# A batched matrix product on one core: the order of the first two loads, and stores joined into three transfers

## The chip, the cores and the metric

The kernel runs on one core of a Trainium2 chip. The metric is the device time of one execution in microseconds (us); the times below are medians of several runs. One execution is also recorded by the hardware profiler; its views are what the text quotes.

## The reference

Thirty-two independent matrix products in float32:

```python
batch, dim_i, dim_j, dim_k = 32, 256, 512, 384
x: (batch, dim_i, dim_j)   y: (batch, dim_j, dim_k)
return np.einsum('bij,bjk->bik', x, y).astype(np.float32)
```

x has 16.8 MB, y 25.2 MB and the result 12.6 MB.

## The kernel before

**Groups.** The 32 products are done in N = 8 groups of Q = 4. Each group uses all 128 partitions: 32 partitions (`PQ`) for each of its four products. One load brings x of a group (2 MB, 16 KB to a partition), one load brings y (3 MB, 24 KB to a partition). Both have two buffers (`x_sb`, `y_sb`). All results of all groups have room of their own in `o_sb`, so that a store never stands in the way of a later group; a group's results are 12 KB to a partition.

**Steps of one group.** GpSimd (POOL in the profile) rounds x and y to 16 bits: x in two halves (`x_r`, line 124), y in two or four pieces (`y_r`, line 132). VectorE (DVE) transposes the rounded x in blocks of 32 (`xt_sb`, line 146). TensorE (PE) multiplies in tiles of 32 rows (line 207), four products side by side, into eight banks of PSUM (`o_ps`): NE = 2 halves of the rows, four banks each. ScalarE (ACT) and VectorE copy the banks into `o_sb` (line 155).

**The order.** All transfers are issued by SyncE (SP) on one queue, in the order of its program. Loads of x(0), y(0), x(1) and y(1) are issued at the start (line 74). For each later group n, SP waits until POOL has rounded both halves of x of group n - 2 and then issues x(n); it waits for the first half of x of group n - 1, which POOL does right after y of group n - 2, and then issues y(n) (lines 97 to 101). Only when all loads are issued does SP come to the stores (lines 102 to 108). The store of a group waits for a mark that PE sets in the second half of the next group, as by then the copies of the group are over; the last store waits for the copies themselves. The last line of SP waits for all the stores.

**POOL's order** is x then y in every group (lines 119 to 133). Before it overwrites a half of `x_r` it waits for `s_free`, with which VectorE says that it has transposed it; before a piece of `y_r`, for PE's marks in the group before. `s_cast` counts the rounded halves of x, `s_yr` the rounded pieces of y.

The functions that the change touches, and what calls them:

Of the kernel before, what the change touches and what calls it, by code (L numbers as in the profile page):

```python
# [11 lines left out]
Q = 4  # L12
NE = 2
STEP = 4
STRAIGHT = 2


@with_exitstack
def kernel(
# [11 lines left out]
    PQ = P // Q  # L31
# [4 lines left out]
    N = B // Q  # L36
    NC = T // STEP

    def sbuf(name, shape, dtype):
        return nc.alloc_sbuf_tensor(name, shape, dtype).ap()  # L40
# [3 lines left out]
    o_sb = sbuf("o_sb", [P, N, NE, H, K], F32)  # L44
# [12 lines left out]
    s_act = nc.alloc_semaphore("s_act")  # L57
    s_dve = nc.alloc_semaphore("s_dve")
    s_pe = nc.alloc_semaphore("s_pe")
    s_sp = nc.alloc_semaphore("s_sp")  # L60
    s_out = nc.alloc_semaphore("s_out")
# [4 lines left out]
    def load_x(n):  # L66
        src = x[n * Q : (n + 1) * Q].rearrange("g (p r) j -> (g p) r j", r=R)
        return nc.sync.dma_start(out=x_sb[n % 2], in_=src).then_inc(s_x[n], 16)

    def load_y(n):  # L70
        src = y[n * Q : (n + 1) * Q].rearrange("g (q t) k -> (g q) t k", t=T)
        return nc.sync.dma_start(out=y_sb[n % 2], in_=src).then_inc(s_y[n], 16)

    for ins in (load_x(0), load_y(0), load_x(1), load_y(1)):
        tc.no_tile_sem_insts.add(ins.ins.name)
    tc.close()
    tc.compile()  # L77
# [9 lines left out]
    def chunk_done(n, e, a):  # L87
        return (n * NE + e) * MARKS + (a + 1 if a < NC - 1 else MARKS)

    sp = nc.sync  # L90

    def store(n):
        dst = out[n * Q : (n + 1) * Q].rearrange("g (s f) k -> (g s) f k", s=PQ)
        src = o_sb[:, n].rearrange("p e h k -> p (e h) k")
        sp.dma_start(out=dst, in_=src).then_inc(s_out, 16)

    for n in range(2, N):
        sp.wait_ge(s_cast, NE * (n - 1))
        load_x(n)
        sp.wait_ge(s_cast, NE * (n - 1) + 1)  # L100
        load_y(n)
    for n in range(N):
        if n < N - 1:
            sp.wait_ge(s_pe, chunk_done(n + 1, NE - 1, 0))
        else:
            sp.wait_ge(s_act, NE)
            sp.wait_ge(s_dve, NE)
        store(n)
    sp.sem_inc(s_sp, 1)
    sp.wait_op(s_out, 16 * N, "sem-ge").then_inc(s_out, -16 * N)  # L110

    def pieces(n):
        w = 1 if n in (0, N - 2, N - 1) else 2
        return [(a, a + w) for a in range(0, NC, w)]

    po = nc.gpsimd
    for n in range(N):
        po.wait_ge(s_x[n], 16)  # L120
        for e in range(NE):
            if n:
                po.wait_ge(s_free, max(2 * n - 2 + e, 1))
            po.tensor_copy(  # L124
                x_r[:, e], x_sb[n % 2][:, e * H : (e + 1) * H]
            ).then_inc(s_cast, 1)
        po.wait_ge(s_y[n], 16)
        for a, b in pieces(n):
            if n:
                po.wait_ge(s_pe, chunk_done(n - 1, NE - 1, b - 1))  # L130
            s = slice(a * STEP, b * STEP)
            ins = po.tensor_copy(y_r[:, s], y_sb[n % 2][:, s])  # L132
            ins.then_inc(s_yr, b - a if b < NC else b - a + NC)
    po.wait_ge(s_sp, 1)
    po.sem_clear(range(nums[0], nums[-1] + 1))

# [48 lines left out]
    def scalar_half(n, e):  # L185
        for g in range(Q - 1):
            a_.wait_ge(s_pe, bank_done(n, e, g))
            blocks = [b for b in BLOCKS[:-OWN] if b[0] == g]
            collect(a_.copy, n, e, blocks, None, s_act if g == Q - 2 else None)
# [3 lines left out]
    a_.sem_inc(s_act, NE)  # L193
    with a_.Fori(0, N - STRAIGHT) as n:
        with a_.Fori(0, NE) as e:
            scalar_half(n, e)
    for n in range(N - STRAIGHT, N):
        for e in range(NE):
# [7 lines left out]
    def product(ps, w, m, start, stop, g):  # L206
        return te.add_instruction(  # L207
            mybir.InstMatmult(
                name=nc.get_next_instruction_name(),
                start_tensor_calc=start,  # L210
                stop_tensor_calc=stop,
                tile_size=(PQ, P),
                tile_position=(PQ * g, 0),
                engine=mybir.EngineType.PE,
                ins=[te.lower_ap(m), te.lower_ap(w)],
                outs=[te.lower_ap(ps)],
            )
        )

    xt = xt_sb.bitcast(MM_DT).rearrange("p t (m c) -> p t m c", c=2)  # L220
    with te.Fori(0, N):
        with te.Fori(0, NE) as e:
            take(s_act)
            take(s_dve)
            for t in range(T):
# [3 lines left out]
                for g in range(Q):  # L229
                    s = slice(g * PQ, (g + 1) * PQ)  # L230
                    ins = product(
                        o_ps[:, e * Q + g, :K],
                        xt[s, t // 2, :, t % 2],
                        y_r[s, t],
                        t == 0,
                        t == T - 1,
                        g,
                    )
# [32 lines left out]
```

## Time and profile before

| | |
|---|---|
| median of three runs | 132.26 us (132.15 to 132.43) |
| the profiled execution | 132.16 us, its span 130.8 us |
| granted clock of TensorE, mean | 0.798 |
| bytes read and written in HBM | 41.94 MB and 12.58 MB |
| transfers issued | 8 of x, 8 of y, 8 of the result |

The span runs from the first to the last instruction; the execution's own time has some more around it. In the profile a row of the timeline has the start, the time from the first to the last of the instructions that it takes together, the engine, the line, the operation, the tile written and the tile read, their number, and in brackets the idle time of the engine before it and what ended that. "SPq" rows are transfers being issued. In a table of stretches the columns are the busy times of PE, PEld (weight load), DVE, ACT and POOL with their numbers of instructions, the granted clock, the mean share in which the 16 DMA engines had a packet, and the rate. A packet is counted where it starts.

### The profile page before, as it was taken

The page shows a single profiled execution, that of the slowest core. Times are in us where ns is not written, and L with a number is a line of the kernel's source. Part 1 is how long each engine was busy: PE and PEld are TensorE (multiplying, and loading weights), DVE is VectorE, ACT ScalarE, POOL GpSimd, SP SyncE. Part 2 cuts the span into 40 slices and gives each one's busy share as a digit, 9 for nine tenths or more (in the row PEclk, how much of TensorE's full clock was granted, in tenths as well). Part 3 has the DMA queues.
Part 4 walks back from the last instruction along what each step waited for, and adds up shares of the span by engine and source line. Part 5 has one row for each costly group of instructions (what it writes and reads, how often), then busy time and mean ns, then how long its engine had stood idle before and what let it go on. Part 6 is the DMA issues. An engine that isn't in the chain of part 4 may idle for free. (4 is left out here: it accounts for less than half of the span.)

```text
span 130.8 us, 3204 instructions
## 1 busy us (share of the span) xinstructions
PE 65.0 (50%) x1024; PEld 53.7 (41%) x1024; DVE 82.7 (63%) x144; ACT 84.3 (64%) x178; POOL 74.2 (57%) x42
## 2 busy tenths in 40 slices
PE   0000069903991698099529915980985499100000
PEld 0000057702990575089329505970963387000000
DVE  0006005897379989966998997589989957920000
ACT  0400000899359989993999899489999967995000
POOL 0047195499919955992899469758964970000000
PEclk9999999996589779756986995599599558965555
DMA  5999999999999999999999999999999999999996
GB/s 105 421 461 406 426 433 466 406 423 436 458 393 431 433 466 398 421 438 458 396 456 413 458 391 453 413 431 421 458 413 405 427 427 428 432 425 428 436 425 263
DMA packets 3459, 54.55 MB, mean 417 GB/s; under 512 B 384, under 2 KB 384, under 8 KB 384
## 3 DMA queue, kind: packets, MB, share of 16 engines
q1 hardware_dynamic: 3456, 54.53, 98.2%
q14 instruction: 3, 0.02, 0.0%
HBM read 41.94 MB, written 12.58 MB: 417 GB/s over the span
## 5 line engine op out<-in xcount | busy, mean ns | idle before, releaser
L155 ACT COPY o_sb<-o_ps (+1 forms) x176 | 82.8, 470 | 31.7 <-PE o_ps L207 29.5
L207 PE MATMUL o_ps<-y_r,xt_sb 32*128 32x384 f16 x1024 | 65.0, 406 | 46.7 <-PEq L204 46.5
L207 PEld LDWEIGHTS o_ps<-y_r,xt_sb 32*128 32x128 f16 x1024 | 53.7, 112 | 57.7 <-issue 52.2
L146 DVE STREAM_TRANSPOSE xt_sb<-x_r 128x256 f32<-128x256 f32 x64 | 38.2, 625 | 31.0 <-PE o_ps L207 20.3
L132 POOL CAST y_r<-y_sb 128x1536 f16<-128x1536 f32 (+1 forms) x22 | 44.3, 2049 | 8.0 <-DMA y_sb<-in_y_dram 7.8
L155 DVE COPY o_sb<-o_ps 32x384 f32 (+1 forms) x80 | 44.5, 557 | 1.6
L124 POOL CAST x_r<-x_sb 128x2048 f16<-128x2048 f32 x16 | 30.2, 1893 | 24.6 <-PE o_ps L207 8.3
L192 ACT ACT_TABLE_LOAD x1 | 1.3, 1283 | 3.5 <-PEq L77 3.5
L255 POOL MEMSET const-float32-0.0<- 128x1 f32 x1 | 0.1, 98 | 0.2 <-issue 0.2
L192 ACT COPY spare<-const-float32-0.0 1x1 f32<-1x1 f32 x1 | 0.2, 190 | 0.0
L255 POOL MEMSET const-bfloat16-1.0<- 128x1 bf16 x1 | 0.1, 101 | 0.0
L255 POOL MEMSET const-uint8-127<- 128x1 uint8 x1 | 0.1, 101 | 0.0
L255 POOL MEMSET const-float32-1.0<- 128x1 f32 x1 | 0.1, 98 | 0.0
## 6 DMA issues: line engine op xcount, KB each, us to landing
y_sb<-in_y_dram SPq DMA_DIRECT2D x8, 3072.0 KB, 16.9
x_sb<-in_x_dram SPq DMA_DIRECT2D x8, 2048.0 KB, 17.4
out_dram<-o_sb SPq DMA_DIRECT2D x8, 1536.0 KB, 24.6
```

Source lines behind the costliest of these rows:

```text
L124: po.tensor_copy(x_r[:, e], x_sb[n % 2][:, e * H : (e + 1) * H]).then_inc(s_cast, 1)
L132: ins = po.tensor_copy(y_r[:, s], y_sb[n % 2][:, s])
L146: v.transpose(xt_w[:, w], words[:, e, w]).then_inc(s_xt, 1)
L155: ins = copy(o_sb[g * PQ : (g + 1) * PQ, n, e, h], o_ps[h * PQ : (h + 1) * PQ, e * Q + g, :K],)
L192: a_.copy(spare, nc.const_aps.tensor(0.0, [1, 1], F32))
L207: return te.add_instruction(mybir.InstMatmult(name=nc.get_next_instruction_name(), start_tensor_calc=start, stop_tensor_calc=stop, tile_si ...
L255: nc = _bacc.Bacc("TRN2", target_bir_lowering=False, num_devices=1)
```

## The change

The first two loads change places: y of group 0 is issued ahead of x of group 0, and POOL rounds y of group 0 ahead of x of group 0. All other groups keep their order. On the side of the stores, the results of groups 0 to 4 go out in one transfer, those of groups 5 and 6 in a second, those of group 7 in a third. The first waits for the mark for which the store of group 4 waited, the second for that of group 6, the third for what the store of group 7 waited for.

```diff
+JOINED = 5
...
-    for ins in (load_x(0), load_y(0), load_x(1), load_y(1)):
+    for ins in (load_y(0), load_x(0), load_x(1), load_y(1)):
...
-    def store(n):
-        dst = out[n * Q : (n + 1) * Q].rearrange("g (s f) k -> (g s) f k", s=PQ)
-        src = o_sb[:, n].rearrange("p e h k -> p (e h) k")
-        sp.dma_start(out=dst, in_=src).then_inc(s_out, 16)
+    def store(first, last):
+        groups = out[first * Q : last * Q].rearrange("(n g) (s f) k -> (g s) n f k", g=Q, s=PQ)
+        src = o_sb[:, first:last].rearrange("p n e h k -> p n (e h) k")
+        sp.dma_start(out=groups, in_=src).then_inc(s_out, 16)
...
-    for n in range(N):
-        if n < N - 1:
-            sp.wait_ge(s_pe, chunk_done(n + 1, NE - 1, 0))
-        else:
-            sp.wait_ge(s_act, NE)
-            sp.wait_ge(s_dve, NE)
-        store(n)
+    sp.wait_ge(s_pe, chunk_done(JOINED, NE - 1, 0))
+    store(0, JOINED)
+    sp.wait_ge(s_pe, chunk_done(N - 1, NE - 1, 0))
+    store(JOINED, N - 1)
+    sp.wait_ge(s_act, NE)
+    sp.wait_ge(s_dve, NE)
+    store(N - 1, N)
     sp.sem_inc(s_sp, 1)
-    sp.wait_op(s_out, 16 * N, "sem-ge").then_inc(s_out, -16 * N)
+    sp.wait_op(s_out, 16 * 3, "sem-ge").then_inc(s_out, -16 * 3)
...
-    for n in range(N):
+
+    def round_x(n):
...
+    def round_y(n):
...
+    round_y(0)
+    round_x(0)
+    for n in range(1, N):
+        round_x(n)
+        round_y(n)
```

## The prediction

> **What bounds the kernel now.** I read the page first, its slices and its queue part.
>
> ```profile
> span 130.8 us, 3204 instructions
> PE 65.0 (50%) x1024; PEld 53.7 (41%) x1024; DVE 82.7 (63%) x144; ACT 84.3 (64%) x178; POOL 74.2 (57%) x42
> ...
> DMA  5999999999999999999999999999999999999996
> ...
> q1 hardware_dynamic: 3456, 54.53, 98.2%
> ...
> y_sb<-in_y_dram SPq DMA_DIRECT2D x8, 3072.0 KB, 16.9
> x_sb<-in_x_dram SPq DMA_DIRECT2D x8, 2048.0 KB, 17.4
> out_dram<-o_sb SPq DMA_DIRECT2D x8, 1536.0 KB, 24.6
> ```
>
> No computing engine is busy for more than two thirds of the span. The row of the DMA engines has a 9 in every slice but the first and the last, and the packets of the one queue fill 98.2% of sixteen engines' span. So the transfers are the bound, and what is left to ask is whether anything in between makes them wait. The chain of waits says the same in a roundabout way: it ends with ACT.
>
> ```profile
> by line: ACT o_sb L155 7.9%; PE o_ps L207 4.2%; issue 0.3%
> 45 pieces in order of time: start us, us, what
> ...
> 118.95 0.47 ACT o_sb L155
> ```
>
> The last piece of computing is over at 118.95 + 0.47 = 119.42 us, 11.4 us before the end of the span, and the chain explains only some 12% of it. The last 11.4 us are transfers that stand in line, the last store behind the earlier ones. A table of stretches shows how well the line is fed (columns: stretch and its length, busy time of the engines, granted clock, DMA share, GB/s).
>
> ```profile
> 0.00:1.70 1.70, 0.00 (x0) 0.00 (x0) 0.00 (x0) 0.00 (x0) 0.20 (x4) 1.00 0.00 0
> 1.70:5.00 3.30, 0.00 (x0) 0.00 (x0) 0.00 (x0) 1.47 (x2) 0.00 (x0) 1.00 1.02 318
> 5.00:28.00 23.00, 8.53 (x128) 6.87 (x128) 8.60 (x15) 4.50 (x10) 12.66 (x8) 1.00 1.00 432
> 28.00:98.00 70.00, 46.09 (x730) 39.26 (x734) 59.24 (x104) 59.47 (x127) 54.24 (x27) 0.78 1.01 431
> 98.00:102.00 4.00, 1.93 (x46) 1.18 (x37) 3.92 (x8) 3.88 (x10) 2.08 (x2) 0.99 0.94 400
> 102.00:118.00 16.00, 8.49 (x128) 6.40 (x128) 10.92 (x19) 13.54 (x30) 5.05 (x4) 0.71 1.01 427
> 118.00:126.00 8.00, 0.00 (x0) 0.00 (x0) 0.00 (x0) 1.40 (x3) 0.00 (x0) 0.50 1.01 430
> 126.00:129.50 3.50, 0.00 (x0) 0.00 (x0) 0.00 (x0) 0.00 (x0) 0.00 (x0) 0.50 1.00 428
> 129.50:130.80 1.30, 0.00 (x0) 0.00 (x0) 0.00 (x0) 0.00 (x0) 0.00 (x0) 0.50 0.05 19
> ```
>
> From 5 to 129.5 us the engines have a share of about 1.0 and carry 427 to 432 GB/s, except for four microseconds at 400 where the loads end and the stores begin. The span is then: 54.53 MB at 431 GB/s, 126.5 us; 1.70 us before the first packet; in 1.70 to 5 us 3.30 x (431 - 318) / 431 = 0.87 us lost to a slow start; by the same sum 0.29 us lost in 98 to 102 and 0.15 us in 102 to 118; and 1.30 x (431 - 19) / 431 = 1.24 us at the end. That makes 130.75 us beside a span of 130.8. The same execution took 132.16 us, 1.36 us more than its span; the median of the runs is 132.26 us, 0.1 above it, so I add or take off what the sum gives at 132.26. The three runs lie 0.28 us apart, about 0.2%: less than 0.26 us can hardly be told from no change here.
>
> **Part one: y of group 0 first.** No byte is added or removed; the first 5 MB come in another order. What could cost time is that work behind them comes later and with it the issues of later loads, since SP sends each only when POOL has rounded what held the buffer. The timeline of before, its rows of SP, POOL, DVE and PE:
>
> ```profile
> 0.74 0.38 SPq L68 DMA_DIRECT2D x_sb<-in_x_dram  x1
> ...
> 8.46 3.72 POOL L124 CAST x_r<-x_sb 128x2048 f16<-128x2048 f32 x2 [8.01 <-DMA x_sb<-in_x_dram]
> ...
> 12.21 0.33 SPq L68 DMA_DIRECT2D x_sb<-in_x_dram  x1
> ...
> 15.74 5.70 POOL L132 CAST y_r<-y_sb 128x1536 f16<-128x1536 f32 x4 [3.56 <-DMA y_sb<-in_y_dram]
> ...
> 17.66 8.53 PE L207 MATMUL o_ps<-y_r,xt_sb 32*128 32x384 f16 x128 [17.66 <-PEq L204]
> 19.66 0.64 DVE L146 STREAM_TRANSPOSE xt_sb<-x_r 128x256 f32<-128x256 f32 x1 [7.07 <-PE o_ps L207]
> ...
> 24.77 3.73 POOL L124 CAST x_r<-x_sb 128x2048 f16<-128x2048 f32 x2 [3.33 <-DVE o_sb L155]
> 26.69 0.33 SPq L72 DMA_DIRECT2D y_sb<-in_y_dram  x1
> ...
> 28.44 5.44 POOL L132 CAST y_r<-y_sb 128x3072 f16<-128x3072 f32 x2
> 28.53 0.33 SPq L68 DMA_DIRECT2D x_sb<-in_x_dram  x1
> ...
> 31.64 8.22 PE L207 MATMUL o_ps<-y_r,xt_sb 32*128 32x384 f16 x128 [5.46 <-PEq L204]
> ...
> 38.61 1.89 POOL L124 CAST x_r<-x_sb 128x2048 f16<-128x2048 f32 x1 [2.89 <-PE o_ps L207]
> ```
>
> In before, x of group 0 is in POOL's hands at 8.46 and y at 15.74. The two together are over at 15.74 whichever is first, since they share one line; y alone takes 15.74 - 8.46 = 7.28 us of it. After: y lands at about 8.46 + (7.28 - 4.9) = 10.9 (4.9 us is the x load, 2.10 MB at 431 GB/s), is rounded in 5.70 us until 16.6, and only then POOL takes x, which landed about 15.7: the halves are done at 18.4 and 20.3. DVE needs 0.64 us for the first transpose, so PE starts near 19.1 instead of 17.66. With all of y rounded it needn't wait for pieces any more; group 1 in before is such a group, and from PE's start to the POOL rounding that waits for its first half it took 38.61 - 31.64 = 6.97 us. So POOL takes x of group 1 at about 26.1 instead of 24.77, 1.3 us later.
>
> Each issue that hangs on this: x of group 2 goes out after both halves of x(0), at 20.3 instead of 12.21 (8.1 us later); y of group 2 after the first half of x(1), at 28.0 instead of 26.69; x of group 3 at 29.9 instead of 28.53; the later ones by at most as much. Do the engines run dry? The four loads sent at the start are 10.49 MB, so they end at about 1.70 + 0.87 + 10.49 / 0.431 = 26.9 us; x(2) at 20.3 is in line 6.6 us before that, and the first load needed 1.70 - 0.74, about 1.0 us, from issue to first packet. x(2) keeps the engines until 26.9 + 4.9 = 31.8; y(2) at 28.0 is 3.8 us early, 2.8 with that 1.0 us. It is hidden, and a slip of 2.8 us beyond the 1.3 would uncover it. Later loads have more cover: y(2) ends at 31.8 + 7.3 = 39.1, and x(3) is sent at 29.9. The compute of later groups waits for its loads (POOL rounds y of group 7 at 101.35 with "DMA y_sb" as the releaser, a row quoted below), so the 1.3 us are taken up on the way.
>
> What no row shows is a start with the bigger packets: 0.87 us are lost in 1.70 to 5 us with x's rows of 16 KB (2048 KB over 128 partitions), and y's rows have 24 KB. If the loss goes with the size, it grows to 1.30 (+0.44); if it goes with the number of packets, each carrying half as much again, it shrinks to 0.58 (-0.29). I take 0, because from 5 us on the rate is 432 with whatever packets are then under way: it looks like a spell of time. Both ends stay for the range.
>
> **Part two: three store transfers instead of eight.** The bytes are the same. SP's waits and issues near the stores, and the work that they wait for:
>
> ```profile
> 84.10 0.33 SPq L72 DMA_DIRECT2D y_sb<-in_y_dram  x1
> 84.47 2.33 SPq L95 DMA_DIRECT2D out_dram<-o_sb  x5
> ...
> 98.01 0.33 SPq L95 DMA_DIRECT2D out_dram<-o_sb  x1
> 109.84 0.33 SPq L95 DMA_DIRECT2D out_dram<-o_sb  x1
> 119.44 0.33 SPq L95 DMA_DIRECT2D out_dram<-o_sb  x1
> 101.35 5.70 POOL L132 CAST y_r<-y_sb 128x1536 f16<-128x1536 f32 x4 [1.92 <-DMA y_sb<-in_y_dram]
> ```
>
> The first five stores go out from 84.47 to 86.80, right behind the last load, and the one transfer of groups 0 to 4 waits for the mark of the fifth, which went out about 86.4: some 2 us later than the first store now. At that time the line holds the rest of y(6), x(7) and y(7), and the loads, 41.94 MB, end at 1.70 + 0.87 + 41.94 / 0.431 = 99.9 us. Cover: 13 us. The second transfer waits for the mark of store 6, at 109.84; groups 0 to 4, 7.86 MB at 428 GB/s, hold the engines from 99.9 until about 118.5, so it is 8.6 us early. Its group 5, which went out at 98.01, gains nothing from that and loses nothing. The third goes at 119.44 as now; groups 5 and 6 hold the line until 118.5 + 7.3 = 125.8, 6.4 us. Nothing else is queued on SP behind these waits, as all loads are sent. The last wait, for the three transfers' completion, ends with the last byte as before.
>
> What can change on the line itself are five boundaries between transfers fewer. No row times one, but stretches bound them: a store of 1.57 MB takes 3.66 us at 430 GB/s, and the stretches with only stores run at 427 to 430 where loads, with fewer boundaries, run at 431 to 432. If all the difference were the boundary, it costs (432 - 430) / 432 x 3.66 = 0.017 us at the least difference and 0.042 us at the largest. Five of them: 0.08 to 0.21 us; nothing, if the difference has another cause. I take 0.08, from the stretch of 118 to 126, where no computing engine disturbs.
>
> The joined transfer has another order of rows. A partition holds 12,288 bytes of each group next to one another, and in memory these lie one group (1.57 MB) apart; the store of one group instead fills memory with neighbouring rows. The Trainium skill's page "DMA: Bandwidth & Descriptors", section "Latency and other measured facts", has rates for copies whose partitions' rows lie at large powers of two: 207 GB/s at 512 KiB and 164 at 2 MiB. No trace here has such an access; an estimate by that page: at 164 GB/s the seven groups' 11.0 MB would take 67 us instead of 25.7. [...]
>
> **Sum.** 130.8 + 0 (start) - 0.08 (boundaries) + 0 (waits, all covered) = 130.7 of span; 132.26 - 0.08 = 132.2 us.
>
> **The rivals.** *Both unknowns help:* -0.29 at the start and -0.21 for the boundaries, 131.76 us. For it speaks that the 0.87 us are lost while few packets are on their way; against it, that the rate of store stretches dips for other reasons (427 while engines compute, 430 when they don't). Chance 0.24, with the milder mixtures past 0.26 us.
>
> *The slow start grows with the packet:* +0.44 - 0.08, 132.62 us, slower than before. It decides as soon as the loss at the start passes 0.87 + 0.34 = 1.21 us. For it: a first packet that creeps has half as many bytes again to creep with. Against it: the rate after 5 us shows nothing of packet size. Chance 0.12.
>
> *The hops between groups slow the stores:* if the two joined transfers, 11.01 MB, go at the 400 GB/s that is the lowest rate of a full line in the table (98 to 102 us), they take 27.5 us instead of 25.7 at 428: +1.8, 134.0 us. It passes 0.26 + 0.08 us at a rate under 423. Chance 0.05; by the skill's rule it would be far more.
>
> *The line runs dry before y(2):* needs the 2.8 us of slip worked out above, and costs what is slipped beyond it; 1 us gives 133.2. Nothing in the rows of PE or POOL is that uneven. Chance 0.03.
>
> *The change does nothing:* the joined transfers cut into the same packets, boundaries for free, 132.26 us; it is inside the forecast.
>
> **How the numbers follow.** Forecast within 0.26 us of before: 0.56, around 132.2 (its own range is 132.0 to 132.5). Faster: 0.24. Slower: 0.12 + 0.05 + 0.03 = 0.20. The range takes in the helped case, 131.7, and the slow start with some spread, 132.8; it leaves out the hops and the dry line.
>
> **What would show it.** Right: a DMA row with 9s throughout, y(2) issued near 28 and x(2) near 20 with no dip of GB/s behind 27 us, three rows of out_dram issued near 86, 110 and 119.5, rates of 427 to 432 in the store stretch. Wrong: under 318 GB/s in 1.7 to 5 us (slow start grows), a store stretch under 423 (hops), a DMA share under 0.9 near 27 or 32 us (dry line), or computing that ends after 125 us, which would uncover the last store.

## The result, and the profile after

The changed kernel takes 131.99 us (median of 11 runs, 131.81 to 132.18) beside 132.39 us of the kernel before (11 runs, 132.15 to 132.58). The ratio is 0.9966, 95% interval 0.9956 to 0.9976: faster by 0.34%, some 0.45 us. Compared once more on the chip of the first experiments it was 0.9972 (0.9961 to 0.9983), 0.37 us. In the five comparisons of this document the kernel before has medians of 132.24 to 132.39 us; the first ratio is to the highest of them.

The two profiles taken with this hardly differ: the profiled executions took 132.16 us before and 132.13 us after, and both spans are 130.8 us. The one of before is a short one of its kind (of 28 executions timed beside the first experiments only four took less than 132.16 us, and the median was 132.28), the one of after the second longest of its eleven. So a difference of 0.4 us can't be read off one pair of profiles; what they do show is whether each step went as told. First the page of after, slices and queue:

```profile
span 130.8 us, 3199 instructions
...
DMA  5999999999999999999999999999999999999995
...
DMA packets 3379, 54.55 MB, mean 417 GB/s; under 512 B 304, under 2 KB 304, under 8 KB 304
...
q1 hardware_dynamic: 3376, 54.53, 98.1%
...
out_dram<-o_sb SPq DMA_DIRECT2D x1, 7680.0 KB, 33.9
out_dram<-o_sb SPq DMA_DIRECT2D x1, 3072.0 KB, 17.3
out_dram<-o_sb SPq DMA_DIRECT2D x1, 1536.0 KB, 11.5
```

The line of transfers is as full as it was. The small packets (under 512 B), of which each transfer has sixteen, are 304 instead of 384: 19 transfers instead of 24. All else is cut as before: the joined stores still go in 12 KB packets, 3,072 packets of data in all.

The timeline of after, its rows of SP, POOL and PE at the start, and SP's stores:

```profile
0.74 0.39 SPq L73 DMA_DIRECT2D y_sb<-in_y_dram  x1
...
10.87 5.69 POOL L136 CAST y_r<-y_sb 128x1536 f16<-128x1536 f32 x4 [10.43 <-DMA y_sb<-in_y_dram]
16.51 3.73 POOL L126 CAST x_r<-x_sb 128x2048 f16<-128x2048 f32 x2
...
19.38 7.41 PE L217 MATMUL o_ps<-y_r,xt_sb 32*128 32x384 f16 x128 [19.38 <-PEq L214]
20.27 0.33 SPq L69 DMA_DIRECT2D x_sb<-in_x_dram  x1
...
25.54 3.73 POOL L126 CAST x_r<-x_sb 128x2048 f16<-128x2048 f32 x2 [5.30 <-DVE o_sb L165]
27.46 0.33 SPq L73 DMA_DIRECT2D y_sb<-in_y_dram  x1
...
29.30 0.33 SPq L69 DMA_DIRECT2D x_sb<-in_x_dram  x1
...
85.85 33.76 SPq L96 DMA_DIRECT2D out_dram<-o_sb  x3
```

y of group 0 is in POOL's hands at 10.87, x(2) goes out at 20.27, y(2) at 27.46, and the first store at 85.85. The last piece of computing starts at 118.78 us:

```profile
118.78 0.47 ACT o_sb L165
```

The stretches of after:

```profile
1.70:5.00 3.30, 0.00 (x0) 0.00 (x0) 0.00 (x0) 1.47 (x2) 0.00 (x0) 1.00 1.05 350
5.00:28.00 23.00, 7.41 (x128) 6.29 (x128) 7.84 (x14) 3.70 (x8) 11.83 (x8) 1.00 0.99 427
28.00:98.00 70.00, 44.00 (x731) 35.22 (x735) 60.27 (x106) 60.36 (x130) 55.28 (x27) 0.80 1.01 431
98.00:102.00 4.00, 1.80 (x45) 1.07 (x33) 3.91 (x8) 3.89 (x9) 1.82 (x2) 1.00 0.98 413
102.00:118.00 16.00, 8.17 (x128) 4.17 (x128) 10.67 (x19) 13.44 (x30) 5.03 (x4) 0.81 1.01 428
118.00:126.00 8.00, 0.00 (x0) 0.00 (x0) 0.00 (x0) 1.22 (x3) 0.00 (x0) 0.50 1.00 427
126.00:129.50 3.50, 0.00 (x0) 0.00 (x0) 0.00 (x0) 0.00 (x0) 0.00 (x0) 0.50 0.98 418
```

The slow start carries 350 GB/s instead of 318, but part of that is counting: a packet counts where it starts, and those of y are half as big again. A fairer stretch ends inside x(1), which stands at the same place in both orders; it follows with the experiments. The two store stretches, 102 to 118 and 118 to 126 us, carry 428 and 427 GB/s; before they carried 427 and 430.

### The profile page after: what moved, and what is told of

Its sections match the earlier page's. It is cut to its first block, busy times and chain, and to the rows that moved or that the text cites. A ratio compares the mean times of both kernels' runs of the same rounds, so it can differ in the third digit from the quotient of the medians.

```text
span 130.8 us, 3199 instructions
## 1 busy us (share of the span) xinstructions
PE 61.4 (47%) x1024; PEld 46.7 (36%) x1024; DVE 82.7 (63%) x144; ACT 84.1 (64%) x178; POOL 74.2 (57%) x42
## 5 line engine op out<-in xcount | busy, mean ns | idle before, releaser
L217 PE MATMUL o_ps<-y_r,xt_sb 32*128 32x384 f16 x1024 | 61.4, 384 | 50.4 <-PEq L214 49.5
L217 PEld LDWEIGHTS o_ps<-y_r,xt_sb 32*128 32x128 f16 x1024 | 46.7, 107 | 64.6 <-issue 56.8
```

Of the source, the lines that this page charges most:

```text
L217: return te.add_instruction(mybir.InstMatmult(name=nc.get_next_instruction_name(), start_tensor_calc=start, stop_tensor_calc=stop, tile_si ...
```

## The experiments

The ratios are to the kernel before on the same chip.

| what | ratio | 95% interval |
|---|---|---|
| loads and rounding of group 0 swapped, eight stores | 0.9983, again 0.9981 | 0.9974 to 0.9993, 0.9966 to 0.9995 |
| three stores, loads as before | 0.9986, 0.9993, 1.0002 | 0.9975 to 0.9998, 0.9980 to 1.0006, 0.9990 to 1.0015 |
| both, the change | 0.9966, again 0.9972 | 0.9956 to 0.9976, 0.9961 to 0.9983 |
| loads swapped, POOL's order as before | 1.0049 | 1.0027 to 1.0071 |
| x(0) in two transfers | 1.0014 | 1.0004 to 1.0024 |
| each store in two, 64 partitions each | 1.0279 | 1.0246 to 1.0312 |
| padding; padding and each store in two | 1.0010; 1.0022 | 0.9996 to 1.0023; 1.0009 to 1.0035 |
| the kernel before itself | 0.9996 | 0.9985 to 1.0008 |

To see differences too small for the runs to tell, I worked out one more thing from the packet records (start, duration and size of every packet of a profiled execution): each transfer ends on each of the sixteen engines with a packet of 4 bytes, so the mean of the sixteen starts of these is the end of a transfer on the mean of the engines. Counted from the first packet, in us:

| kernel | first two loads done | from there to the last load | stores | last engine behind the mean at the end |
|---|---|---|---|---|
| before, two profiles | 13.27, 13.19 | 85.31, 85.34 | 29.42, 29.42 | 0.56, 0.95 |
| three stores, three profiles | 13.25, 13.28, 13.27 | 85.32, 85.32, 85.31 | 29.39, 29.39, 29.39 | 0.68, 0.65, 0.62 |
| loads swapped, two profiles | 13.07, 13.06 | 85.31, 85.31 | 29.42, 29.42 | 0.43, 0.71 |
| both, two profiles | 13.17, 13.12 | 85.31, 85.31 | 29.38, 29.39 | 0.67, 0.62 |

**Loads only.**

```diff
-    for ins in (load_x(0), load_y(0), load_x(1), load_y(1)):
+    for ins in (load_y(0), load_x(0), load_x(1), load_y(1)):
...
+    round_y(0)
+    round_x(0)
+    for n in range(1, N):
+        round_x(n)
+        round_y(n)
```

> y of group 0 first in loads and rounding; eight stores as before. Theory START (the bigger packets lose less while the transfers get going): the whole gain is here, about -0.4 us against the kernel before, and the stretch 1.7 to 5 us carries near 350 GB/s instead of 318. Theory BOUNDARIES (fewer gaps between transfers): nothing here, within 0.1 us of before. Half each: -0.2 us.

> Both loads and POOL's order of group 0 swapped, eight stores, a second time. Theory START: -0.2 us again against before, 1.7 to 5 us at 350 GB/s, and the first two loads done 0.1 to 0.2 us earlier on the mean of the engines. If the first figure was chance, within 0.1 us of before.

Measured: -0.17% and -0.19%, or 0.22 and 0.25 us, both clear of no change. The stretch from the first packet into x(1), of before, of the second profile of before, and of the two profiles with the loads swapped:

```profile
1.70:17.00 15.30, 0.00 (x0) 0.00 (x0) 2.21 (x4) 1.47 (x2) 4.99 (x3) 1.00 1.01 407
```

```profile
1.70:17.00 15.30, 0.00 (x0) 0.00 (x0) 2.21 (x4) 1.47 (x2) 4.96 (x3) 1.00 1.01 411
```

```profile
1.70:17.00 15.30, 0.00 (x0) 0.00 (x0) 0.00 (x0) 1.47 (x2) 6.08 (x5) 1.00 1.01 411
```

```profile
1.70:17.00 15.30, 0.00 (x0) 0.00 (x0) 0.00 (x0) 1.47 (x2) 6.14 (x5) 1.00 1.01 410
```

One GB/s more over this stretch is 15 KB, 0.036 us. The start of before varies by 4 GB/s from one execution to the next, and the swapped ones lie at its upper end; the two profiles of the whole change carry 408 and 410 GB/s. So this stretch decides nothing. The table has it finer: in all eight profiles in which x is loaded first by one transfer, the first two loads are done at 13.19 to 13.30, mean 13.25 us; in the five in which y is, at 13.06 to 13.17, mean 13.10. So 0.15 us of the 0.24 are shown at the start. From there on the loads take 85.31 us in either order.

The records also show where the start loses its time: in one long packet or two to an engine. Once the line runs, a 16 KB packet takes 0.61 us and a 24 KB packet 0.91 us; of a kernel's first load, 15 to 22 packets took longer, up to 2.01 and 2.30 us. Summed up and divided by the sixteen engines, the packets of the first load take 0.82 to 0.96 us more than at the usual pace when x comes first (eight profiles, mean 0.89), and 0.71 to 0.80 us when y does (five profiles, mean 0.76).

**Stores only.**

```diff
-    for n in range(N):
-        if n < N - 1:
-            sp.wait_ge(s_pe, chunk_done(n + 1, NE - 1, 0))
...
-        store(n)
+    sp.wait_ge(s_pe, chunk_done(JOINED, NE - 1, 0))
+    store(0, JOINED)
+    sp.wait_ge(s_pe, chunk_done(N - 1, NE - 1, 0))
+    store(JOINED, N - 1)
...
+    store(N - 1, N)
```

> x of group 0 first as before; stores in three transfers. Theory BOUNDARIES: the whole gain is here, about -0.4 us against the kernel before, 0.08 us for each of five boundaries. Theory START: within 0.1 us of before. Half each: -0.2 us.

> Stores in three transfers, loads as before, a second time on the same runs of before as the next ones. Theory BOUNDARIES as the two comparisons so far have it (-0.15 us by itself, -0.19 us on top of the loads): -0.17 us. Theory TRACE (what the records of all engines say: 0.007 us for each of five boundaries): -0.03 us, inside the interval around no change.

> Stores in three transfers, loads as before, a third time, since the first two gave 0.9986 and 0.9993 with intervals that hold both theories. Theory BOUNDARIES: 0.9990 or less again, -0.14 us. Theory TRACE: 0.9998, -0.03 us; in the records the stores take 29.39 us on the mean of the engines instead of 29.42.

The first comparison alone would have given the stores half of the gain. The three together have a mean of 0.9994, 0.08 us, and two of the three intervals hold no change, so the runs don't show that the stores gain anything. The records are steadier: 29.39 us instead of 29.42 in every profile, 0.033 us for five boundaries.

**The price of a boundary, doubled.** The first try cut each store by partitions:

```diff
-        sp.dma_start(out=dst, in_=src).then_inc(s_out, 16)
+        for c in range(2):
+            rows = slice(c * P // 2, (c + 1) * P // 2)
+            sp.dma_start(out=dst[rows], in_=src[rows]).then_inc(s_out, 16)
...
```

> The kernel before with every store cut into two transfers of 64 partitions: the same packets of 12 KB, eight boundaries more. Theory BOUNDARIES at 0.08 us each: +0.64 us. Theory START: no change, within 0.1 us. With my forecast's price of 0.017 us: +0.14 us.

Measured: +2.8%, 3.7 us, nearly six times what the dearer theory gave. The stretches of the stores in its profile:

```profile
102.00:110.00 8.00, 6.27 (x87) 2.99 (x91) 5.78 (x11) 5.81 (x14) 5.25 (x4) 0.79 1.01 331
110.00:118.00 8.00, 1.96 (x49) 1.19 (x37) 4.91 (x9) 7.80 (x17) 0.00 (x0) 0.79 1.01 419
118.00:126.00 8.00, 0.00 (x0) 0.00 (x0) 0.00 (x0) 1.12 (x3) 0.00 (x0) 0.50 1.00 424
```

The engines are busy all the time (1.01) and yet move 331 GB/s for 8 us: there are no gaps, but a 12 KB packet lasts 0.595 us on the mean of that stretch where it lasts 0.465 in before. So the run doesn't test what it was made for. The next try has as many boundaries with all partitions in each transfer and loses next to nothing, so the loss goes with the halves of the partitions; by what it comes about, and why it wears off after some transfers, wasn't tried. The Trainium skill's page "DMA: Bandwidth & Descriptors", section "Rules for kernel authors", advises against two transfers to disjoint halves of the partitions, as they share the same engines either way. This run agrees, and here they were not only no faster but slower by 2.8%.

The second try keeps all partitions and cuts by the halves of a group's rows. To have equal packets on both sides, the results are padded first:

```diff
-    o_sb = sbuf("o_sb", [P, N, NE, H, K], F32)
+    o_pad = sbuf("o_sb", [P, N, NE, H * K + 16], F32)
+    o_sb = o_pad[:, :, :, : H * K].rearrange("p n e (h k) -> p n e h k", h=H)
...
-        dst = out[n * Q : (n + 1) * Q].rearrange("g (s f) k -> (g s) f k", s=PQ)
-        src = o_sb[:, n].rearrange("p e h k -> p (e h) k")
-        sp.dma_start(out=dst, in_=src).then_inc(s_out, 16)
+        dst = out[n * Q : (n + 1) * Q].rearrange("g (s e h) k -> (g s) e (h k)", s=PQ, e=NE)
+        src = o_sb[:, n].rearrange("p e h k -> p e (h k)")
+        for e in range(NE):
+            sp.dma_start(out=dst[:, e], in_=src[:, e]).then_inc(s_out, 16)
...
```

The run with padding alone has the same lines without the loop over `e`.

> The kernel before with 64 bytes of padding behind each half of a group's results in o_sb, so that a store's packets are 6 KB and twice as many; still eight stores. It is the base for the next run. If packets cost what the records show between 12 KB and 24 KB (some ns each), 64 more packets on each engine cost 0.2 to 0.6 us; what it is compared with is the next kernel, not before.

> The same packets of 6 KB, but every store issued as two transfers, one for each half: sixteen stores, eight boundaries more than the run with padding alone, all 128 partitions in each. Theory BOUNDARIES (0.03 us each, from -0.14 us for five): 0.22 us more than with padding alone. Theory TRACE (0.007 us each): 0.05 us more, not to be told from nothing.

Padding alone comes to +0.10%, 0.13 us, with no change inside its interval; in the records its stores take 29.71 us on the mean of the engines instead of 29.42, so 64 packets more on each engine cost 0.29 us, 0.0046 us each. In twice as many transfers they take 29.75 us: eight boundaries cost 0.037 us, 0.005 us each. A boundary adds one 4-byte packet to each engine, and by these two figures it costs about what any other packet more does. The stretch of 102 to 126 us, with padding alone and cut, says the same in its last column:

```profile
102.00:126.00 24.00, 7.85 (x128) 5.56 (x128) 11.37 (x20) 15.36 (x33) 5.36 (x4) 0.74 1.02 424
```

```profile
102.00:126.00 24.00, 8.26 (x128) 4.27 (x128) 10.66 (x19) 14.70 (x32) 5.26 (x4) 0.70 1.02 423
```

The medians, 132.48 and 132.66 us, are 0.18 us apart, nearer to the 0.22 of theory BOUNDARIES; with twelve runs each they scatter too much to tell 0.04 from 0.22. So theory TRACE stands on the records alone: on the mean of the engines a boundary costs some 0.005 to 0.007 us. Whether boundaries also hold up the last engine these runs don't settle.

**POOL's order.** The first load swapped, but POOL rounds x(0) first as before, and eight stores:

> Only the issue of the first two loads is swapped; POOL rounds x of group 0 ahead of y of group 0 as before, and the stores are as before. Theory START: the first transfer alone makes the gain, -0.2 us, as with both swapped. Theory COMPUTE (what the later and denser start of PE does to traffic and clock): the gain belongs to POOL's order, so this is within 0.1 us of before. Computing starts later by POOL's 5.7 us for y of group 0; the loads stay covered in both.

Both theories were wrong: +0.49%, 0.65 us slower. I had written that the loads stay covered; they don't. Its timeline:

```profile
15.86 3.73 POOL L124 CAST x_r<-x_sb 128x2048 f16<-128x2048 f32 x2 [15.42 <-DMA x_sb<-in_x_dram]
...
19.54 5.71 POOL L132 CAST y_r<-y_sb 128x1536 f16<-128x1536 f32 x4
...
28.31 3.74 POOL L124 CAST x_r<-x_sb 128x2048 f16<-128x2048 f32 x2 [3.06 <-DVE o_sb L155]
30.23 0.33 SPq L72 DMA_DIRECT2D y_sb<-in_y_dram  x1
```

POOL lets y lie, which lands at about 10.9, and works only from 15.86; y(2) goes out at 30.23. Three stretches of this kernel:

```profile
30.00:32.00 2.00, 0.00 (x0) 0.00 (x0) 1.97 (x4) 1.95 (x5) 2.00 (x3) 1.00 1.24 475
32.00:34.00 2.00, 0.00 (x0) 0.00 (x0) 1.93 (x5) 1.94 (x5) 2.00 (x2) 0.83 0.85 356
98.00:101.00 3.00, 3.00 (x48) 1.92 (x40) 2.93 (x6) 2.92 (x7) 1.57 (x1) 0.53 0.97 351
```

The same three of before:

```profile
30.00:32.00 2.00, 0.36 (x3) 0.30 (x3) 1.96 (x4) 1.95 (x5) 2.00 (x2) 0.55 1.08 463
32.00:34.00 2.00, 2.00 (x30) 1.86 (x30) 0.40 (x2) 1.95 (x5) 2.00 (x2) 0.50 1.06 455
98.00:101.00 3.00, 1.93 (x46) 1.18 (x37) 2.93 (x7) 2.92 (x8) 1.43 (x1) 1.00 0.91 384
```

The share of 0.85 in 32 to 34 us looks like the line running dry, the rival of the prediction. But a packet counts where it starts, and the 2 us before have 1.24. By the records at least fifteen of the sixteen engines have a packet at every moment from 28 to 40 us; one has none for 0.5 us, which is 0.03 us on the mean. What is lost is lost in packets that last longer: 13 of the 128 of y(2) took 1.03 to 1.82 us instead of 0.91, as the first packets of a kernel do, and y(2) ends 0.3 us later than with POOL's order swapped too. Here y(2) was issued 1.27 us ahead of its first packet (31.50 us); in the profile of after it was 4.2 us ahead (31.65 us), and none of its packets took over 0.92 us. That the short lead is what makes them long is likely but wasn't tried. Another 0.45 us or so is lost at the end of the loads, where 21 packets of y(7) took 1.0 to 1.94 us; what does that I don't know.

This run shows why the change swaps POOL's order too. The start itself is as quick as with both swapped, 13.06 us for the first two loads, so that part of the gain doesn't hang on POOL. Theory COMPUTE for the rest of the gain isn't settled by it, as this kernel loses time elsewhere.

**Smaller first packets.**

```diff
+    def load_x0(c):
+        r = slice(c * H, (c + 1) * H)
+        src = x[0:Q].rearrange("g (p r) j -> (g p) r j", r=R)
+        return nc.sync.dma_start(out=x_sb[0][:, r], in_=src[:, r]).then_inc(s_x[0], 16)
...
-    for ins in (load_x(0), load_y(0), load_x(1), load_y(1)):
+    for ins in (load_x0(0), load_x0(1), load_y(0), load_x(1), load_y(1)):
...
-        po.wait_ge(s_x[n], 16)
+        po.wait_ge(s_x[n], 16 if n else 32)
```

> The kernel before with x of group 0 loaded by two transfers of half its rows, so that the first packets have 8 KB instead of 16 KB; everything else as before. Theory START in its form 'the loss goes with the number of packets under way, not with bytes': the slow start grows, +0.2 to +0.5 us, and the stretch 1.7 to 5 us carries less than 318 GB/s. In its form 'a spell of fixed time': no change, within 0.1 us, and the first packet's size is not what made the gain.

Measured: +0.14%, 0.19 us by the ratio, in the direction of packets, at the low edge of its figure. But its profile doesn't show the reason I gave:

```profile
1.70:5.00 3.30, 0.00 (x0) 0.00 (x0) 0.00 (x0) 0.79 (x1) 0.00 (x0) 1.00 0.93 323
1.70:17.00 15.30, 0.00 (x0) 0.00 (x0) 2.21 (x4) 1.47 (x2) 5.00 (x3) 1.00 1.00 412
```

323 and 412 GB/s are not under before's 318 and 407. The records go further: the 8 KB packets of x(0) lost only 0.62 us at the start, and the first two loads were done at 13.07 us, as early as with y first. If the loss went with the number of packets, it should have doubled. So "more packets, slower start" is contradicted by this profile, and so is "the bigger the first packet, the quicker": the loss is 0.62 us with 8 KB, 0.89 with 16 KB and 0.76 with 24 KB. On the mean of the engines this execution ended its stores 127.91 us after the first packet, before's two ended at 128.00 and 127.95; but its last engine came 1.12 us behind the mean, and the span is 131.3 us. From the first two loads to the last it took 85.44 us where the others of x first took 85.31 to 85.39. It was the longest of its eleven executions; why their median is 0.19 us above before stays open.

**The null and the change again.**

> The kernel before under a name of its own: a null, and a second profile of it. Ratio 1.000 with an interval of about 0.1% to each side. If the first profile of before (span 130.8 us) was one of the early ones, this one has a span near 131.0 us. Mean over the sixteen engines of the end of the stores, counted from the first packet: 128.0 us by both theories; only the last engine's end differs from run to run.

> The changed kernel once more on the chip of the other runs, for a second profile and an interval beside theirs: -0.4 us against the kernel before by both theories; if the gain belongs to one chip alone, another figure. Last engine's end against the mean rate at the end tells whether the profile of the first run was one of the late ones.

The null came out as expected, and its profile has a span of 131.2 us where the first had 130.8, with the stores of both at 29.42 us on the mean of the engines. The end of the second profile of before:

```profile
126.00:129.50 3.50, 0.00 (x0) 0.00 (x0) 0.00 (x0) 0.00 (x0) 0.00 (x0) 0.50 0.96 411
129.50:131.20 1.70, 0.00 (x0) 0.00 (x0) 0.00 (x0) 0.00 (x0) 0.00 (x0) 0.50 0.07 29
```

411 GB/s instead of 428 in the last stretch, and 1.7 us with hardly a packet: most engines are done and three come late, at 130.23, 130.38 and 130.66 us, where the last one of the first profile came at 130.32. That is the 0.4 us between two executions of one program, as much as the change is worth. The change again: -0.28%, a span of 130.6 us.

## Why the prediction was right or wrong

**The bound and the cover: right.** The line of transfers stayed full. The forecast had x(2) at 20.3 (measured 20.27), y(2) at 28.0 (27.46), x(3) at 29.9 (29.30) and the first store at about 86.4 (85.85). PE began at 19.38 where the forecast had 19.1. The computing ended at 118.78 + 0.47 = 119.25 us, 0.17 us earlier than before.

**The cover of y(2): too large by 0.6 us or more, and the price was of another kind.** I allowed y(2) a slip to 30.8 us. In the run with POOL's old order it went out at 30.23, and 0.3 us were lost at once, though the engines were not left without packets: y(2)'s first packet started at 31.50, as soon as the first engine was through with x(2). The prediction knew only a line that runs dry, not a transfer whose packets last longer. Its sign for the dry line, a share under 0.9 near 32 us, can't tell the two apart. The change itself stays clear of this.

**The start: the term that was mis-sized.** I put 0, "a spell of time", and kept -0.29 as the lower end. The 0.87 us that I read off the rate of before are 0.89 by the packets. Measured with the loads alone: -0.22 and -0.25 us, nearer to the end that I had kept than to my pick. In the records it is -0.13 us by the packets of the first load and -0.15 us by the end of the first two, halfway between the two. The other 0.1 us remains unexplained: the last engine is 0.69 us behind the mean with x first (two profiles of before, three with three stores) and 0.61 us with y first (four), and single profiles differ by more than that. That -0.29 came out so near is luck, as its reason was that the loss goes with the number of packets: by that rule the 8 KB packets of the run with x(0) in two transfers should have lost 2 x 0.87 = 1.74 us, and they lost 0.62. What makes the start quicker with y first stays open.

**The boundaries: right in size, or high.** I took 0.08 us for five. The runs give 0.08 on the mean of three comparisons, not clear of nothing; the records give 0.033 us. The joined stores still ran at 428 and 427 GB/s where the loads ran at 431, so most of that difference, from which I had worked out the price, isn't the boundary.

**The joined order of rows: no cost, as the sum has it.** No row ahead of the forecast showed that such an access keeps its rate, and the sum simply has nothing for it. The runs show it: with rows one group apart the stores run at 428 and 427 GB/s. The Trainium skill's rates for rows at large powers of two (page "DMA: Bandwidth & Descriptors", section "Latency and other measured facts") have no counterpart in this access: a group is 1.5 MiB, no power of two, and the rows of neighbouring partitions stay 12 KB apart as before.

**The likeliest case: wrong, the range right.** By the runs of the parts the sum should have been -0.24 - 0.08 = -0.32 us; the change measured -0.45 and -0.37, with intervals that reach down to -0.32 and -0.22. That is past the 0.26 us that I called no change (against the 132.26 us on which the sum was built it is 0.27), and the case it belongs to is "both unknowns help" at 131.76 us, to which I gave 0.24. The result lies in the range because the range took that case in. By the runs it is mostly the start's term that I had too small; but of the whole gain the records show only a part. On the mean of the engines the two profiles of the change end 127.87 and 127.82 us after the first packet and those of before 128.00 and 127.95: 0.13 us. The other 0.24 to 0.32 us are not explained. The rival of a slow start that grows with the packet is ruled out by the loads alone.

## What to carry to other kernels

When the transfers fill the span, only what stands at the two ends is left to win: how quickly the first ones get going and how late the last engine finishes. Joining transfers that stand in line anyway gained some nanoseconds for each here; swapping the first load gained more, some 0.2 us, and lost 0.65 us where the work that frees its buffers was not swapped with it. And a gain of the size of one execution's scatter is seen only over many executions: two profiles of one program were as far apart here as the two programs.

## What the runs showed that I had not expected

- Between transfers queued one behind the other, a boundary costs 0.005 to 0.007 us on the mean of the engines.
- Stores of 64 partitions each, one after the other, ran at 331 GB/s for 8 us with engines busy throughout, and cost 3.7 us in all.
- At the end the last of sixteen engines is 0.4 to 1.2 us behind their mean (1.8 us with the stores of 64 partitions), and this differs from one execution to the next: 0.56 and 0.95 us in two profiles of before.
- The slow start of a kernel's transfers is one long packet or two to an engine, and its cost doesn't follow the size of the packets: 0.62 us with 8 KB (one profile), 0.89 with 16 KB, 0.76 with 24 KB.
